# Splitting the products with the values into a high and a low step, with new figures in the plan that orders a two-layer attention kernel

## The chip, the cores and the metric

The kernel runs on one core of a Trainium2 chip. The metric is the device time of one execution in microseconds (us). Timed runs come without a profile; one further execution is recorded by the hardware profiler, and all stretches and durations below are of that one. Engines: PE is TensorE, PEld its weight loads, ACT ScalarE, DVE VectorE, POOL GpSimd, SP SyncE, which issues the DMAs.

## The reference, cut to what matters

Two layers over 1024 tokens of width 1024. Each normalises its input, multiplies it with one combined input weight, runs three groups of attention heads side by side, gates and concatenates their outputs, multiplies with an output weight, normalises and adds the residual.

```python
for l in range(DEPTH):
    h = rms_norm(x, pre_norm[l])
    (dq, dk, dv, dgate, gq, gk, gv, ggate, mq, mgate) = jnp.split(h @ w_in[l], IN_OFFSETS, axis=-1)
    oa = diff_attention(...)   # 6 heads: (softmax(q1 k1) - lam * softmax(q2 k2)) @ v
    ob = gqa_attention(...)    # 6 q heads on 2 kv heads: softmax(q k) @ v
    om = softmax(mq mk) @ mv   # 4 heads into 256 memory tokens
    y = jnp.concatenate([oa, ob, om], axis=-1) @ w_out[l]
    x = x + rms_norm(y, post_norm[l])
```

## The kernel before, in words

All large products are made of split operands: a number is kept as a high part and a low part, and high x high, high x low and low x high are added in PSUM. The softmax weights are split too. A unit is one PSUM tile of 128 x 1024 scores (pp). ScalarE takes its exponential into e (line 853, float32), ScalarE (rarely VectorE) rounds that to the high part eh (lines 857 and 858, float16), and GpSimd or VectorE subtracts to get the low part el (VectorE 859, GpSimd 860; the plan picks whichever it thinks is done first). Then `pv_part` multiplies with the values: for each block of 128 keys three products of 64 or 65 columns, eh with the values' high part (line 504), eh with the values' low part (505), el with the values' high part (506). The weights of each product are loaded anew. `pv_part` waits until all of its units have both parts, takes one 512-wide PSUM bank (ps), issues all its products as one piece of work, and ScalarE copies the result out (line 949).

An item is one head: "d" items (12 a layer, differential; units on line 1036), "g" items (6; units on 1250 and 1251) and "m" items (4, into the memory tokens; units on 1304 and 1305). Before an item's units the row maxima are needed: products on line 1026 (d), 1238 and 1239 (g) or 1293 and 1294 (m), reduced by VectorE on line 897, transposed on line 872, written by lines 878 and 879 and sent into the query operand by DMA. The m items share one pair of query operands, so the next m item's operands are fetched by DMA (big<-s_mqa, big<-s_gqb) only after the last unit of the m item before. The d items run beside the rest of the input projection (line 493), the g and m items after them, then the output product (line 1394).

The order on each engine is not the chip's choice. While the program is built, a plan in Python plays the kernel through: `use` gives each piece of work a duration on an engine, `LAT` a delay until others see its end, `KINDS` says how many PSUM tiles of each size each kind of work may hold and with which priority; a piece is written into the program at the moment at which the plan starts it. Each engine then runs its instructions strictly in that order. A changed figure in the plan thus reorders the whole program.

## Time and profile before

| | us |
|---|---|
| median of 3 runs | 1551.15 (1551.09 to 1554.43) |
| profiled execution | 1553.02 |
| its span, first to last instruction | 1551.2 |
| PE busy | 1487.1 |
| DVE, POOL, ACT busy | 1036.2, 903.0, 896.5 |

The profiled execution is 1.8 us longer than its span and 1.9 us longer than the median. PE's busy time is a union of overlapping products whose ends are modelled, so it is an upper bound of its work. PEclk is the granted TensorE clock as a share of 2.4 GHz: 1.00 is that, 0.50 is 1.2 GHz.

### The profile page before, as it was taken

The numbers are of one execution on the slowest core, as the hardware profiler recorded it, in microseconds if no ns is written. First come the engines' busy times: TensorE is split into PE (matmuls) and PEld (weight loads), VectorE is DVE, ScalarE is ACT, GpSimd is POOL, SyncE is SP. The second block draws the span as 40 slices with busy tenths as digits, with TensorE's granted clock in tenths as the row PEclk, the third lists the DMA queues.
The fourth block names the chain that finished last, engine by engine and source line by source line (L and its number), as shares of the span: only waits on it lengthen the run. The fifth ranks groups of instructions, "written<-read, shape, count | busy, mean of one in ns | idle before, by whom it ended". The sixth has DMA issues, their size and how long they took to land. (4 is left out here: it accounts for less than half of the span.)

```text
span 1551.2 us, 39344 instructions
## 1 busy us (share of the span) xinstructions
PE 1487.1 (96%) x15920; PEld 1375.1 (89%) x15920; DVE 1036.2 (67%) x2042; ACT 896.5 (58%) x1428; POOL 903.0 (58%) x647
## 2 busy tenths in 40 slices
PE   6999999999999999999999999999999998899997
PEld 5999999989999888888889999999899998788886
DVE  7747776788865886825566487776887757777143
ACT  4332668767668576673333346677657657576511
POOL 4133668789768486561122257678887757585500
PEclk9999999999999998999999999999999999899999
DMA  6435223233323644215254523223332156332242
GB/s 203 134 106 152 77 77 103 71 96 94 95 82 84 175 117 100 57 49 199 94 163 133 137 83 97 80 59 103 111 104 63 56 144 174 79 84 70 83 147 95
DMA packets 166048, 163.97 MB, mean 106 GB/s; under 512 B 14853, under 2 KB 140357, under 8 KB 165866
## 3 DMA queue, kind: packets, MB, share of 16 engines
q1 hardware_dynamic: 165866, 161.46, 35.7%
q8 instruction: 125, 2.05, 0.6%
q14 instruction: 57, 0.47, 0.1%
HBM read 110.96 MB, written 50.09 MB: 104 GB/s over the span
## 5 line engine op out<-in xcount | busy, mean ns | idle before, releaser
L860 POOL TENSOR_TENSOR el<-e,eh 128x1024 f16<-128x1024 f32 x258 | 570.0, 2221 | 208.0 <-ACT eh L857 194.7
L897 DVE TENSOR_REDUCE mx<-ps 128x1 f32<-128x512 f32 (+1 forms) x608 | 404.6, 684 | 145.6 <-PE ps L1026 86.8
L493 PE MATMUL ps<-wt,big 128*128 128x256 f32 x3456 | 490.0, 285 | 2.0 <-DVE nat L606 1.7
L493 PEld LDWEIGHTS ps<-wt,big 128*128 128x128 f32 x3456 | 465.0, 190 | 18.8 <-ACT e L853 2.0
L853 ACT ACTIVATE e<-pp 128x1024 f32<-128x1024 f32 x304 | 309.3, 1024 | 108.2 <-PE pp L1251 61.9
L857 ACT ACTIVATE eh<-e 128x1024 f16<-128x1024 f32 x262 | 275.4, 1057 | 2.4
L504 PEld LDWEIGHTS <-eh 128*128 128x128 f16 x2144 | 195.0, 96 | 14.4 <-issue 10.9
L394 POOL TENSOR_TENSOR wt<-rt,wt 128x512 fp32r<-128x512 f32 x89 | 123.7, 1401 | 136.6 <-ACT wt L392 96.0
L506 PEld LDWEIGHTS <-el 128*128 128x128 f16 x2144 | 196.6, 99 | 3.8 <-POOL el L860 3.4
L505 PEld LDWEIGHTS <-eh 128*128 128x128 f16 x2144 | 196.6, 97 | 0.7 <-issue 0.5
L436 POOL TENSOR_SCALAR u<-ss 128x1 f32<-128x1 f32 (+3 forms) x96 | 23.9, 249 | 253.3 <-DVE ss L1478 109.0
L493 PE MATMUL pp<-wt,big 128*128 128x256 f32 x1152 | 156.5, 291 | 8.8 <-POOL wt L394 4.1
L1026 PE MATMUL ps<-sdk,sdq 96*128 96x512 f32 x384 | 158.2, 413 | 3.9 <-DVE mx L897 2.4
L493 PEld LDWEIGHTS pp<-wt,big 128*128 128x128 f32 x1152 | 144.6, 194 | 11.7 <-POOL wt L394 4.9
L504 PE MATMUL ps<-vd,eh 128*128 128x65 f16 x1536 | 150.3, 193 | 0.2
L505 PE MATMUL ps<-vd,eh 128*128 128x64 f16 x1536 | 149.5, 194 | 0.0
L506 PE MATMUL ps<-vd,el 128*128 128x65 f16 x1536 | 149.0, 192 | 0.0
L1036 PE MATMUL pp<-sdq,sdk 98*128 98x256 f32 x768 | 125.8, 286 | 0.0
L1036 PEld LDWEIGHTS pp<-sdq,sdk 98*128 98x128 f32 x768 | 112.5, 190 | 5.3
L1250 PE MATMUL pp<-big 128*128 128x256 f32 x384 | 102.6, 297 | 0.3 <-ACT e L853 0.3
L1251 PE MATMUL pp<-big 67*128 67x256 f32 x384 | 100.3, 291 | 1.5 <-DMA big<-nl 1.5
L949 ACT ACTIVATE o<-ps 128x130 f32<-128x130 f32 (+1 forms) x160 | 46.1, 288 | 92.7 <-PE ps L506 91.8
(243 smaller groups left out, 2829.4 us busy)
## 6 DMA issues: line engine op xcount, KB each, us to landing
rt<-in_w_in SPq DMA_DIRECT2D x48, 256.0 KB
rt<-in_w_in SPq DMA_DIRECT2D x96, 128.0 KB
gt<-g_scr SPq DMA_DIRECT2D x32, 256.0 KB
rt<-in_w_out SPq DMA_DIRECT2D x32, 256.0 KB
sdq<-s_dqa SPq DMA_DIRECT2D x48, 128.0 KB
sdk<-s_dka SPq DMA_DIRECT2D x48, 128.0 KB
big<-s_gqa SPq DMA_DIRECT2D x24, 256.0 KB
big<-s_gqb SPq DMA_DIRECT2D x24, 256.0 KB
```

Source lines behind the costliest of these rows:

```text
L394: (POOL(512, lambda: pool.tensor_sub(out=lo, in0=rt, in1=raw(hi))), W_BIAS[1]))
L493: pe.matmul(ps, lhsT=x[:, kt, :], rhs=y[:, a, :], start=(kt == 0 and n == 0), stop=(kt == KT - 1 and n == 2))
L504: pe.matmul(o[:, 0:65], lhsT=eh, rhs=v[:, kt, 0:65], start=(kt == 0), stop=False, skip_group_check=True)
L505: pe.matmul(o[:, 0:64], lhsT=eh, rhs=v[:, kt, 66:130], start=False, stop=False, skip_group_check=True)
L506: pe.matmul(o[:, 0:65], lhsT=el, rhs=v[:, kt, 0:65], start=False, stop=(kt == n - 1), skip_group_check=True)
L853: yield ACT(1024, lambda: act.activation(e, ps, AF.Exp, scale=scale), 0, "p")
L857: yield either((ACT(1024, lambda: act.activation(eh, e, AF.Copy)), 0.0), (DVE(1024, lambda: dve.tensor_copy(out=eh, in_=e), 0, fast=True, ...
L860: (POOL(1024, lambda: pool.tensor_sub(out=el, in0=e, in1=eh)), 0.0))
L897: yield DVE(512, lambda: dve.tensor_reduce(out=out_ap, in_=src, axis=AX.X, op=ALU.max), MXP[0])
L1026: yield (512, lambda ps, n=n: pe.matmul(ps, lhsT=q()[0:96, i * P:(i + 1) * P], rhs=k()[0:96, n * 512:(n + 1) * 512], start=True, stop=True ...
L1036: pe.matmul(ps[:, a * 256:(a + 1) * 256], lhsT=k()[0:98, kt * P:(kt + 1) * P], rhs=q()[0:98, j * 256:(j + 1) * 256], start=True, stop=True)
L1250: pe.matmul(o, lhsT=ka()[:, ks], rhs=a()[:, qs], start=True, stop=False)
```

## The change

`attend` now makes either the two products with eh or the one with el. `pv_part` waits for the high parts alone, takes its bank, issues all high products of its query blocks, then waits for the low parts, and issues the low products as a second piece of work, with a priority (`PVL`, 0.1) ahead of the first's (`PVP`, 0.2). Since the blocks of one bank are now open at the same time, only the first product of the bank starts an accumulation. The kind "pv" may hold two banks in place of one, and `exp_part` fires one event for the high part and one for the low. The number of products and of weight loads is unchanged.

The plan's figures change: ScalarE's fixed part per instruction falls from 0.17 or 0.2 to 0.05 or 0.095 us, VectorE's from 0.13 to 0.08, PE's rate goes from 2210 to 2175 columns a us with small corrections for three kinds of work, and the plan now doubles PE's durations while its own account of PE's work says that the clock is low (`clocked`).

```diff
-DVE_FIX = 0.13
-PV_N = 2
+DVE_FIX = 0.08
+PV_AT, PVL = 0, 0.1
+PE_RATE, CLOCK_WINDOW, CLOCK_LOW, CLOCK_HIGH = 2175.0, 3.41, 0.33, 0.85
-KINDS = {... 'pv': (1, 1, 1), ...}
+KINDS = {... 'pv': (1, 2, 1), ...}
...
+        if eng == "pe":
+            dur = self.clocked(dur)
...
+    def clocked(self, dur):
+
+        while self.window < int(self.t / CLOCK_WINDOW):
+            share = self.work / CLOCK_WINDOW
+            self.half = share < (CLOCK_HIGH if self.half else CLOCK_LOW)
+            self.window += 1
+            self.work = max(0.0, self.work - CLOCK_WINDOW)
+        dur *= 2.0 if self.half else 1.0
+        self.work += dur
+        return dur
...
-        return use("pe", ncols / 2210.0, fn, prio, lat)
+        return use("pe", ncols / PE_RATE, fn, prio, lat)
...
-        return use("act", (0.2 if src == "s" else 0.17) + n / 1200.0, fn, prio)
+        return use("act", (0.095 if src == "s" else 0.05) + n / 1200.0, fn, prio)
...
-    def attend(o, v, es):
+    def attend(o, v, es, low, first):
...
+        for kt, e in enumerate(es):
+            if low:
+                pe.matmul(o[:, 0:65], lhsT=e, rhs=v[:, kt, 0:65], start=False, stop=(kt == n - 1),
+                          skip_group_check=True)
+            else:
+                pe.matmul(o[:, 0:65], lhsT=e, rhs=v[:, kt, 0:65], start=(first and kt == 0), stop=False,
+                          skip_group_check=True)
+                pe.matmul(o[:, 0:64], lhsT=e, rhs=v[:, kt, 66:130], start=False, stop=False, skip_group_check=True)
...
             for e in evs:
-                yield wait(e)
+                yield wait(e[PV_AT])
...
-            yield PE(sum(c for _, c in some) + 100, lambda: [f() for f, _ in some], PVP)
+            yield PE(sum(c for _, c in some) * 2 / 3 + 50, lambda: [f(0) for f, _ in some], PVP, 0.0)
+            for e in evs:
+                yield wait(e[1])
+            yield PE(sum(c for _, c in some) / 3 + 50, lambda: [f(1) for f, _ in some], PVL)
```

Two places in PE's order show it. The first is in layer 0, where units of the second m item (lines 1304 and 1305; 1330 and 1331 after) stand beside the products of a g item with the values (vg). Before, the three kinds of product alternate:

```order
L1305 MATMUL pp_75<-big 128x512
L504 LDWEIGHTS eh_1531
L504 MATMUL ps_78<-vg,eh_1531 128x65
L505 LDWEIGHTS eh_1531
L505 MATMUL ps_78<-vg,eh_1531 128x64
L506 LDWEIGHTS el_1532
L506 MATMUL ps_78<-vg,el_1532 128x65
```

Here and now the last high product (527), the unit with row maxima of a g item on either side of it (1264, 1265), and the first low product (522) of the same bank, ps_80:

```order
L527 LDWEIGHTS eh_1540
L527 MATMUL ps_80<-vg,eh_1540 128x64
L1264 MATMUL ps_79<-big 128x512
L1265 MATMUL ps_79<-big 128x512
L1330 MATMUL pp_75<-big 128x512
L1331 MATMUL pp_75<-big 128x512
L1330 MATMUL pp_75<-big 128x512
L1331 MATMUL pp_75<-big 128x512
L1264 MATMUL ps_77<-big 128x512
L1265 MATMUL ps_77<-big 128x512
L522 LDWEIGHTS el_1539
L522 MATMUL ps_80<-vg,el_1539 128x65
```

Eight products of 512 columns came between the parts of one group that stood together before. The second place, also on PE in layer 0, is where the row maxima of the fourth m item begin (1293 and 1294; 1319 and 1320 after). Before, they follow a g unit (1250, 1251), and both groups of products of the third m item with its values stand ahead of them:

```order
L1250 MATMUL pp_76<-big 128x256
L1251 MATMUL pp_76<-big 128x256
L1293 MATMUL ps_77<-big 128x256
L1294 MATMUL ps_77<-big 128x256
L1293 MATMUL ps_77<-big 128x256
```

Now the high products of the first such group, `vm` with ehm, and one g unit (1276, 1277) stand right ahead of them; its low products and the second group come later:

```order
L527 LDWEIGHTS ehm_8505
L527 MATMUL ps_79<-vm,ehm_8505 128x64
L1276 MATMUL pp_75<-big 128x256
L1277 MATMUL pp_75<-big 128x256
L1276 MATMUL pp_75<-big 128x256
L1277 MATMUL pp_75<-big 128x256
L1276 MATMUL pp_75<-big 128x256
L1277 MATMUL pp_75<-big 128x256
L1276 MATMUL pp_75<-big 128x256
L1277 MATMUL pp_75<-big 128x256
L1319 MATMUL ps_80<-big 128x256
L1320 MATMUL ps_80<-big 128x256
```

The row maxima moved forward, past half of the work that stood ahead of them. Counted over the whole program, VectorE makes 49 of the 304 low parts (16 before) and GpSimd 255 (288 before).

## Rows read from the trace of the kernel before

**Rows 1.** The page, its first part: busy time, share of the span and instructions of each engine.

```profile
PE 1487.1 (96%) x15920; PEld 1375.1 (89%) x15920; DVE 1036.2 (67%) x2042; ACT 896.5 (58%) x1428; POOL 903.0 (58%) x647
```

**Rows 2.** The page, its second part: busy tenths of PE and granted clock in 40 slices of 38.8 us.

```profile
PE   6999999999999999999999999999999998899997
...
PEclk9999999999999998999999999999999999899999
```

**Rows 3.** Who PE waited for over the whole span, longest first: us in total, times, longest.

```profile
PE ps L456 <- DVE xt L476: 8.2, 2, 5.4
PE ps L506 <- POOL elm L860: 6.5, 7, 1.8
PE pp L493 <- POOL wt L394: 4.1, 4, 1.6
PE pp L493 <- DVE nat L606: 4.0, 6, 1.2
PE ps L506 <- POOL el L860: 3.2, 2, 1.6
...
PE ps L1294 <- DMA big<-s_mqa: 2.8, 2, 2.1
PE ps L1026 <- DVE mx L897: 2.4, 2, 1.2
PE pp L1686 <- DMA grow<-in_pre_norm: 2.3, 1, 2.3
PE ps L1294 <- DMA big<-s_gqb: 2.0, 3, 1.1
...
PE ps L1293 <- DMA big<-s_mqa: 0.8, 2, 0.6
...
PE ps L1293 <- DMA big<-s_gqb: 0.4, 1, 0.4
```

**Rows 4.** Busy time of each engine by stretch (us from the span's start): length, then PE, PEld, DVE, ACT and POOL busy with counts, the granted clock, the DMA share and GB/s.

```profile
250.00:540.00 290.00, 286.41 (x3559) 272.48 (x3558) 215.45 (x406) 197.55 (x303) 220.70 (x149) 1.00 0.35 99
578.00:583.20 5.20, 2.12 (x50) 1.68 (x48) 3.37 (x4) 1.55 (x4) 2.27 (x2) 1.00 1.02 236
583.23:593.47 10.24, 10.24 (x41) 9.25 (x42) 5.82 (x13) 3.10 (x3) 1.53 (x1) 0.50 0.33 74
1298.00:1303.40 5.40, 3.81 (x74) 3.60 (x73) 5.40 (x6) 5.11 (x9) 4.94 (x3) 1.00 0.59 189
1303.44:1306.85 3.41, 3.41 (x47) 3.22 (x44) 2.46 (x3) 1.13 (x2) 3.41 (x2) 0.50 0.65 215
1306.90:1317.10 10.20, 7.49 (x105) 6.43 (x104) 4.43 (x6) 9.36 (x14) 7.97 (x5) 1.00 0.67 147
1317.10:1320.50 3.40, 3.40 (x18) 3.40 (x17) 2.65 (x5) 0.00 (x0) 2.45 (x2) 0.50 1.02 240
1342.00:1347.80 5.80, 3.73 (x99) 3.27 (x98) 5.14 (x5) 2.88 (x5) 4.04 (x2) 1.00 0.78 184
1347.82:1358.05 10.23, 9.10 (x37) 8.31 (x38) 5.06 (x10) 2.20 (x3) 0.29 (x1) 0.50 0.43 104
```

**Rows 5.** PE in order of time around the second m item of layer 0: start, us, engine, line, out<-in, shape, and in brackets the idle time before it.

```profile
573.76 0.20 PE L504 MATMUL ps<-vg,eh 128*128 128x65 f16 x1
...
575.20 0.19 PE L506 MATMUL ps<-vg,el 128*128 128x65 f16 x1
575.23 0.48 PE L1304 MATMUL pp<-big 128*128 128x512 f32 x1
...
576.01 0.39 PE L1305 MATMUL pp<-big 67*128 67x512 f32 x1
576.24 0.20 PE L504 MATMUL ps<-vg,eh 128*128 128x65 f16 x1
...
578.88 0.19 PE L504 MATMUL ps<-vm,ehm 128*128 128x65 f16 x1
580.99 0.19 PE L505 MATMUL ps<-vm,ehm 128*128 128x64 f16 x1
...
582.10 0.35 PE L1293 MATMUL ps<-big 128*128 128x256 f32 x1 [0.35 <-DMA big<-s_gqb]
583.20 0.58 PE L1294 MATMUL ps<-big 65*128 65x256 f32 x1 [0.74 <-DMA big<-s_gqb]
```

**Rows 6.** ACT and, last, POOL in order of time in the same stretch.

```profile
576.50 1.02 ACT L853 ACTIVATE e<-pp 128x1024 f32<-128x1024 f32 x1 [0.66 <-PE pp L1305]
577.55 1.06 ACT L857 ACTIVATE ehm<-e 128x1024 f16<-128x1024 f32 x1
...
578.74 2.12 POOL L860 TENSOR_TENSOR elm<-e,ehm 128x1024 f16<-128x1024 f32 x1 [0.59 <-ACT ehm L857]
```

**Rows 7.** PE in order of time elsewhere: the last unit of the first and third m items of layer 0 and of the first of layer 1 (1305), and the second operand's product of the next m item (1294).

```profile
546.37 0.40 PE L1305 MATMUL pp<-big 67*128 67x512 f32 x1
...
553.66 0.39 PE L1294 MATMUL ps<-big 65*128 65x256 f32 x1 [0.69 <-DMA big<-s_mqa]
...
611.86 0.40 PE L1305 MATMUL pp<-big 67*128 67x512 f32 x1
...
620.17 0.39 PE L1294 MATMUL ps<-big 65*128 65x256 f32 x1 [1.10 <-DMA big<-s_gqb]
...
1307.98 0.40 PE L1305 MATMUL pp<-big 67*128 67x512 f32 x1
...
1316.70 0.39 PE L1294 MATMUL ps<-big 65*128 65x256 f32 x1 [2.09 <-DMA big<-s_mqa]
```

**Rows 8.** Groups by line: count | busy us, mean ns of one | idle before it, and what ended it. ACT, POOL and DVE.

```profile
L392 ACT ACTIVATE wt<-rt 128x512 fp32r<-128x512 f32 x128 | 78.0, 627 | 15.7 <-DMA rt<-in_w_in 8.8 <-PE ps L493 2.2 <-PE pp L493 2.0
...
L860 POOL TENSOR_TENSOR el<-e,eh 128x1024 f16<-128x1024 f32 x258 | 570.0, 2221 | 208.0 <-ACT eh L857 194.7 <-POOL el L860 3.2 <-PE ps L1026 3.0
...
L859 DVE TENSOR_TENSOR el<-e,eh 128x1024 f16<-128x1024 f32 x10 | 15.7, 1570 | 12.0 <-POOL el L860 8.3 <-ACT eh L857 3.8
L859 DVE TENSOR_TENSOR elm<-e,ehm 128x1024 f16<-128x1024 f32 x6 | 12.1, 2025 | 0.0
```

**Rows 9.** ACT and PE in order of time at the start of the program: three ACT instructions of one line in a row, and 24 and 10 products of line 493 in a row.

```profile
8.01 1.66 ACT L392 ACTIVATE wt<-rt 128x512 fp32r<-128x512 f32 x3
...
23.44 3.12 PE L493 MATMUL pp<-wt,big 128*128 128x256 f32 x24
...
26.75 1.44 PE L493 MATMUL pp<-wt,big 128*128 128x256 f32 x10
```

More of the change, by code (lines that the diff above doesn't have):

```diff
@@ L74 @@
 LAT = {"pe": 0.231, "act": 0.176, "dve": 0.165, "pool": 0.121, "hwdge": 0.65, "dma": 0.95}
-DVE_FIX = 0.13
-PV_N = 2
+DVE_FIX = 0.08
+PV_AT, PVL = 0, 0.1
 X_GATE, XT = 2, 4
 DMA_RATE = 300.0
+PE_RATE, CLOCK_WINDOW, CLOCK_LOW, CLOCK_HIGH = 2175.0, 3.41, 0.33, 0.85
 SLACK = 0.8
-KINDS = {'un': (0.5, 2, 2), 'z': (1, 2, 2), 's0': (2, 2, 2), 's1': (0, 2, 2), 'st': (1, 4, 1), 'pv': (1, 1, 1), 'tr': (-1, 2, 1), 'mx': (2, 4, 1), 'zh': (3, 2, 1)}
+KINDS = {'un': (0.5, 2, 2), 'z': (1, 2, 2), 's0': (2, 2, 2), 's1': (0, 2, 2), 'st': (1, 4, 1), 'pv': (1, 2, 1), 'tr': (-1, 2, 1), 'mx': (2, 4, 1), 'zh': (3, 2, 1)}
 def raw(t):
@@ L192, in __init__ @@
         self.port = {"dve": 0.0, "pool": 0.0}
+        self.window, self.work, self.half = 0, 0.0, False
         self.live = 0
@@ L494, in f @@
                                   stop=(kt == KT - 1 and n == 2))
-            yield PE(6 * NC, f, prio, None if j == 3 else 0.0)
+            yield PE(6 * NC * 1.015, f, prio, None if j == 3 else 0.0)
             if last and wi is not None:
                 free("wt", wi)
-    def attend(o, v, es):
+    def attend(o, v, es, low, first):
         n = len(es)
-        for kt, (eh, el) in enumerate(es):
-            pe.matmul(o[:, 0:65], lhsT=eh, rhs=v[:, kt, 0:65], start=(kt == 0), stop=False, skip_group_check=True)
-            pe.matmul(o[:, 0:64], lhsT=eh, rhs=v[:, kt, 66:130], start=False, stop=False, skip_group_check=True)
-            pe.matmul(o[:, 0:65], lhsT=el, rhs=v[:, kt, 0:65], start=False, stop=(kt == n - 1),
-                      skip_group_check=True)
+        for kt, e in enumerate(es):
[6 more added lines that the diff above has]
+                pe.matmul(o[:, 0:64], lhsT=e, rhs=v[:, kt, 66:130], start=False, stop=False, skip_group_check=True)
     class Layer:
@@ L858, in exp_part @@
                          (DVE(1024, lambda: dve.tensor_copy(out=eh, in_=e), 0, fast=True, port=True), HI_BIAS[kind]))
+            box.append((eh, el, ei))
+            ev[0].fire(pl)
             yield either((DVE(1024, lambda: dve.tensor_sub(out=el, in0=e, in1=eh), port=True), LO_BIAS[kind]),
@@ L861, in exp_part @@
             free("e32", n32[1])
-            box.append((eh, el, ei))
-            ev.fire(pl)
+            ev[1].fire(pl)
         def nm_rows(mx, n2, scale, dst, ready):
@@ L972, in stream @@
                     yield PE(ncols, lambda: mm(ps), UNP)
-                    box, ev = [], Event()
+                    box, ev = [], (Event(), Event())
                     pl.spawn(exp_part(ps, slot, it.scale, kind, box, ev, (e32, k)))
@@ L992, in pv_list @@
                     es.append((eh[:, o:o + P], el[:, o:o + P]))
-                out.append((lambda c=66 * i, es=es: attend(ps[:, c:c + 65], v, es), 201 * nk))
+                out.append((lambda low, c=66 * i, es=es: attend(
+                    ps[:, c:c + 65], v, [e[low] for e in es], low, c == 0), 198 * nk))
             return out
@@ L1037, in f @@
                                   rhs=q()[0:98, j * 256:(j + 1) * 256], start=True, stop=True)
-                return 1024, f
+                return 1040, f
             it.loads, it.max_parts, it.unit_mm = loads, max_parts, unit_mm
@@ L1397, in z_mm @@
                         end = k == KT_ORDER[-1] and h == 1
-                        yield PE(3 * 512, f, prio, None if end else 0.0)
+                        yield PE(3 * 512 * 0.98, f, prio, None if end else 0.0)
                         used.append(t)
```

## The prediction

> **What bounds the kernel now.** First the busy times: PE is busy for 1487.1 of the span's 1551.2 us, no other engine for more than 67% [rows 1]. So the kernel is bound by PE's work, and the change, which leaves the number of products and weight loads as it is, can only win what PE loses: 1551.2 - 1487.1 = 64.1 us of idle time, and what PE loses inside its busy time at the lower clock. The slices show where: PE is at six tenths in the first one, and the only two with a clock below nine tenths of full, at 582 and 1318 us, lie once in each layer, in the stage of the g and m items; the second of them and its neighbour are also the only ones before the end with PE at eight tenths [rows 2]. Third, whom PE waits for: the low parts el of the softmax weights for 6.5 + 3.2 = 9.7 us in nine waits; the query operands of the m items for 2.8 + 2.0 + 0.8 + 0.4 = 6.0 us; at the program's start normalised input and the gain for 8.2 + 2.3 = 10.5 us; the rest is spread over many waits, weight parts and rotated projections the longest of them [rows 3]. Fourth, the stretches: four at the granted clock 0.50 (1.2 GHz), 583 to 593, 1303 to 1307, 1317 to 1321 and 1348 to 1358; in front of each PE was busy for 41% to 73% only, while in a d stage, 250 to 540, it was busy for 286.4 of 290 us and the clock stayed at 1.00 [rows 4].
>
> **The change part by part.** Durations first. A product of 256 columns takes (3.12 - 1.44)/14 = 0.12 us from start to start [rows 9], one of 512 columns 576.24 - 576.01 = 0.23 us, one with the values 0.031 us (48 of them take 575.23 - 573.76 = 1.47 us) [rows 5]. With these I count how much PE work stands in an order between two places; PE's own idle time there comes on top, so the counts are lower bounds of the distances.
>
> *The wait for el.* The place to see it: PE is through with the last product of a unit of the second m item at 576.24, its exponential starts at 576.50, the high part is done at 577.55 + 1.06 = 578.61, the low part on GpSimd at 578.74 + 2.12 = 580.86, and PE, which stopped after 578.88, goes on at 580.99 [rows 5, 6]. So with nothing in the way el can be used 580.99 - 576.24 = 4.75 us after its unit, and eh, with the same 0.1 us of handing over, 2.5 us after it. In PE's old order 14 of the 160 groups stand closer than 4.75 us behind their unit, the closest 2.3 us. In the new one three low steps do (4.69 us in each layer, 2.84 us once): 0.1 + 1.9 = 2.0 us are left. The high steps are new waits: three of 160 stand closer than 2.5 us (2.22 us in each layer, 1.85 us once), 1.1 us in all. This term: -9.7 + 2.0 + 1.1 = -6.6 us; bounds -9.7 and, if the high steps wait as the low ones did, 0.
>
> *The clock.* The four stretches at 0.50 hold 10.24 + 3.41 + 3.40 + 9.10 = 26.15 us of busy PE [rows 4], half of which full clock would save: 13.1 us. Ahead of the first stands the wait for el above, 2.1 us; but waits for the m operands stand there too (583.20 in [rows 5], 1316.70 in [rows 7]), and those the change does not touch. I take half, -6.5 us; bounds -13.1 and 0.
>
> *The m operands.* From the start of the last product of an m item's units to the second operand's product of the next item, PE took 7.3, 7.2 and 8.3 us in layer 0 and 8.7 us in the first case of layer 1 [rows 5, 7]: the DMAs start only after that unit, whatever else PE does. Take 7.2, less 0.23 for that product and 0.12 for the first operand's, 6.85 us of other work to be found. The old order has 4.8, 3.0 and 5.8 us, the new one 4.6, 6.2 and 3.9 (the last: 48 high and 16 low products, and two g units of eight products of 256 columns). That leaves 2.2 + 0.6 + 2.9 = 5.7 us of waiting a layer, 11.5 in all, where 6.0 is waited now [rows 3]: **+5.5 us**; bounds 0 (PE idles in between for other reasons, as it did for el) and +9 (8.3 in place of 7.2 us in three of six).
>
> *The plan's figures.* Three ScalarE instructions of 0.627 us [rows 8] take 1.66 us in a row [rows 9], (1.66 - 0.63)/2 = 0.52 from start to start. The old figure for them is 0.2 + 512/1200 = 0.63, the new one 0.095 + 0.43 = 0.52: the old plan held ScalarE busy 0.1 us too long with every instruction, the new one does not. Orders laid out on true times should make PE wait less at places where it now waits for ACT, DVE and POOL. The idle time outside el, m operands and start is 64.1 - 9.7 - 6.0 - 10.5 = 37.9 us. No row shows what a better figure wins, and at the layer seams and the end there is no other work to put in; I take -2 us, a twentieth. Bounds: -12, a third of it, and +8, since tighter distances leave less room for what the plan has no figure of, DMA and the port that DVE and POOL share by the plan's own account (el on DVE takes 1570 to 2025 ns here, POOL's 2221 [rows 8]).
>
> *Edits at no cost.* The 33 low parts that go from POOL to DVE add 33 x 1.74 = 57 us to DVE and take 33 x 2.22 = 73 us from POOL; neither sets the end [rows 1]. What queues behind them on DVE is the reduction of the row maxima; PE waits 2.4 us for it now [rows 3], and four small banks cover more; uncovered, that wait again, +2.4. The second bank does nothing in steady work: in the new order high and low steps strictly alternate, since a group still waits for the one before it; it only spares the wait for ScalarE's copy out of the first. The start of the program is reordered too (ScalarE squares the first tile before it copies the gain, VectorE makes more of the input tiles ahead of the low parts): 0, within 3 us either way, of the 8.2 us there [rows 3].
>
> The sum against the profiled execution: 1553.0 - 6.6 - 6.5 + 5.5 - 2.0 = 1543.4 us. The median of the runs is 1.9 us below the profiled execution, so the forecast for the median is **1541.5 us**, 0.6% faster.
>
> **The rivals.**
>
> *The high step waits for ScalarE (slower).* In the d stages ScalarE is busy for 197.6 of 290 us [rows 4]. If one of its other instructions stands in the way, eh comes not 2.5 but 3 to 3.5 us after the unit (one rounding of 1.06 us [rows 6] in its way). Summed over the new order, PE waits 1.1 us for the high parts if they take 2.5 us, 8 us at 3.0 and 25 us at 3.5: the gain of 9.6 us is gone from about 3.1 us on, and at 3.5 the time is 1541.5 + 24 = 1565. For it: 46 of the 96 high steps of the d items stand within 4 us of their unit, where the closest group stood 5.5 us off before. Against it: the plan lets a high step start only when its own ScalarE is done, and its figure for that engine now agrees with the rows.
>
> *The waits change places (no change).* The el waits shrink by 6.6 us, the m operands take 5.5 more, and since it is those that stand in front of the low stretches, the clock falls as often as now: 1553.0 - 6.6 + 5.5 = 1551.9, less 1.9, 1550. For it: the last DMA wait ends 0.03 us before the stretch at 583.23 [rows 4, 5].
>
> *The figures matter more (much faster).* All four low stretches go (-13.1), the better distances win 12 us, and the m operands cost what the sum above has: 1553.0 - 6.6 - 13.1 + 5.5 - 12 = 1526.8, less 1.9, 1525.
>
> *The clock falls at the new seams (slower).* Each group now has a seam between two steps at which PE can stand for a moment. The trace so far speaks against it: in the d stage the groups follow one another through the four small banks at 1.00 [rows 4]. If it happened at three seams a layer, each time for 10.24 us as at 583 and losing half of them, it would cost 6 x 5.1 = 31 us: 1541.5 + 31 = 1572; for 3.4 us each, 10 us: 1552. The Trainium skill, "TensorE: Matmul & The Clock Gate", section "A second HAM failure mode: psum-queue depth-cycling", has a rule that speaks for this rival: a kernel that cycled its products through PSUM banks idled so often between groups that its clock went back and forth between the two levels. By that rule the second bank and the split harm; by the row above, cycling banks did not harm here as long as the work was there.
>
> **How the numbers follow.** A measurement of this kernel can tell about 0.3% from no change, so faster is below 1546.5 and slower above 1555.8. The forecast, with its own range 1534 to 1550, gets 0.48, of which 0.40 faster, 0.07 the same and 0.01 slower; waits that change places 0.19 (0.02, 0.13, 0.04); much faster 0.17; the high step 0.12; the seams 0.04. That makes 0.59 faster, 0.20 the same, 0.21 slower. The range of 1527 to 1558 leaves out half of the much faster case and most of the two slower ones, some 0.2; the bounds of the terms (clock -13.1, operands +9, figures -12 to +8) fill it.
>
> **What would show it.** In the profile after, the waits of the low products for el should come to some 2 us, those of the high products for eh to less; if the high ones are above 10 us, the first rival holds. The waits of lines 1319 and 1320 for the m operands should be near 11 us. Of the four stretches at 0.50 about half should be gone. PE's busy time should fall by the clock's share alone, some 6 us, to about 1480, with the same 15920 products; more idle time at the layer seams or in the d stages than now would prove the term of the figures wrong.

## The result, and the profile after

| | before | after |
|---|---|---|
| median, us | 1552.79 (4 runs, 1551.09 to 1555.79) | 1572.85 (4 runs, 1572.26 to 1572.92) |
| ratio | | 1.0126, interval 1.0107 to 1.0145 |
| span of the profiled execution, us | 1551.2 | 1571.1 |

The change makes the kernel 20 us slower; 1541.5 us had been forecast, 0.6% faster, and the range ended at 1558. After each line of before stands its new number here: 456, 493, 1026, 1238, 1293, 1294 and 1686 [rows 3] are 472, 509, 1052, 1264, 1319, 1320 and 1712; the products with the values are 525 and 527 (high parts) and 522 (low parts).

The page of after, its first part and PE's row of the second:

```profile
PE 1505.9 (96%) x15920; PEld 1377.7 (88%) x15920; DVE 1059.4 (67%) x2079; ACT 892.2 (57%) x1428; POOL 830.2 (53%) x610
...
PE   6999999999999999999989999999999998999997
```

With the same 15920 products PE is busy 18.8 us longer than in [rows 1], where some 6 us less were expected: the first sign that PE's own work had become dearer. The idle time, 1571.1 - 1505.9 = 65.2 us, hardly moved from 64.1. Whom PE waited for in after, over the whole span (us in total, times, longest):

```profile
PE ps L472 <- DVE xt L492: 9.7, 4, 4.2
PE ps L509 <- DVE nat L626: 6.1, 4, 1.6
PE ps L472 <- DVE hn L492: 5.2, 2, 3.7
PE ps L1264 <- DVE gs L711: 4.0, 2, 2.5
PE ps L509 <- DVE nl L901: 3.5, 2, 1.8
PE ps L1319 <- DMA big<-s_gqb: 3.0, 2, 1.9
...
PE ps L1320 <- DMA big<-s_gqb: 1.6, 2, 0.9
...
PE ps L1320 <- DMA big<-s_mqa: 1.0, 2, 0.5
...
PE ps L525 <- ACT ehm L878: 0.7, 2, 0.4
...
PE ps L522 <- DVE el L882: 0.2, 1, 0.2
```

The 9.7 us of waits for low parts [rows 3] are down to 0.2, and the waits for high parts come to 0.7. The m operands cost 3.0 + 1.6 + 1.0 = 5.6 us, as much as before (6.0). In their place stand waits for VectorE: for rotated projections (nat), the normalised input of layer 1 (hn), gates (gs) and row maxima (nl). All rows of this view that name VectorE add up to 42.4 us; in the trace of before they add up to 23.7.

Now PE in order of time in layer 0 (start, us, line, out<-in, shape): the end of a high step, four products of a unit, the low step, and the next unit.

```profile
560.09 0.19 PE L527 MATMUL ps<-vg,ehm 128*128 128x64 f16 x1
560.12 0.48 PE L1330 MATMUL pp<-big 128*128 128x512 f32 x1
560.43 0.40 PE L1331 MATMUL pp<-big 67*128 67x512 f32 x1
560.67 0.40 PE L1330 MATMUL pp<-big 128*128 128x512 f32 x1
560.91 0.40 PE L1331 MATMUL pp<-big 67*128 67x512 f32 x1
561.15 0.66 PE L522 MATMUL ps<-vg,elm 128*128 128x65 f16 x16
561.65 0.48 PE L1330 MATMUL pp<-big 128*128 128x512 f32 x1
561.97 0.40 PE L1331 MATMUL pp<-big 67*128 67x512 f32 x1
```

The first 512-column product behind value products takes 560.43 - 560.12 = 0.31 us to the next start, the second and third 0.24; behind the low step again 0.32. No engine is waited for there. It is a price for the seam itself, about 0.08 us, and the split makes a group pay it about twice.

To add up such prices I took, for every product of a trace, the time from its start to the next start, less the median for its shape in the trace of before, and sorted these excesses by place. Products in the first 20 us and at the low clock are kept apart; elsewhere an excess above 0.15 us counts as a wait, whatever the place.

| excess of PE, us | before | after | difference |
|---|---|---|---|
| float32 product behind a value product | 10.2 (122 places) | 21.7 (260) | +11.5 |
| value products among themselves | -0.1 | 5.3 | +5.4 |
| first value product of a group | 1.5 | 3.1 | +1.6 |
| waits above 0.15 us | 58.8 | 61.1 | +2.3 |
| at the low clock | 16.3 | 12.9 | -3.4 |
| behind transposes, start, all else | 24.6 | 27.1 | +2.5 |
| sum | 111.3 | 131.2 | +19.9 |

The sum is the 20 us that the span grew by. This is bookkeeping on two traces: what each part does to the time when it alone is taken away, the experiments below have to tell. The first three rows, 18.5 us, are what I call PE's own time below; the other two that matter are waits and low clock.

### The profile page after: what moved, and what is told of

Its sections match the earlier page's. It is cut to its first block, busy times and chain, and to the rows that moved or that the text cites. A ratio compares the mean times of both kernels' runs of the same rounds, so it can differ in the third digit from the quotient of the medians.

```text
span 1571.1 us, 39318 instructions
## 1 busy us (share of the span) xinstructions
PE 1505.9 (96%) x15920; PEld 1377.7 (88%) x15920; DVE 1059.4 (67%) x2079; ACT 892.2 (57%) x1428; POOL 830.2 (53%) x610
## 3 DMA queue, kind: packets, MB, share of 16 engines
q8 instruction: 125, 2.05, 0.6%
## 4 chain that ended last, share of the span: by engine, by line
PE 72%; DVE 10%; DMA 6%; issue 5%; ACT 3%; POOL 2%; SPq 1%; POOLq 0%; ACTq 0%; DVEq 0%
PE ps L509 21%; PE pp L1420 8%; PE pp L509 5%; PE ps L1052 5%; PE pp L1062 5%; PE ps L522 4%; PE ps L525 4%; PE ps L527 4%; DVE mx L919 3%; PE ps L1264 2%; PE pp L1276 2%; PE pp L1277 2%; PE ps L1265 2%; SPq L346 1%; PE ps L1420 1%
## 5 line engine op out<-in xcount | busy, mean ns | idle before, releaser
L883 POOL TENSOR_TENSOR el<-e,eh 128x1024 f16<-128x1024 f32 x235 | 516.1, 2210 | 182.5 <-ACT eh L878 156.8
L509 PE MATMUL ps<-wt,big 128*128 128x256 f32 x3456 | 495.6, 287 | 11.6 <-DVE nat L626 6.1
L874 ACT ACTIVATE e<-pp 128x1024 f32<-128x1024 f32 x304 | 309.5, 1027 | 126.2 <-PE pp L1062 65.9
L410 POOL TENSOR_TENSOR wt<-rt,wt 128x512 fp32r<-128x512 f32 x81 | 114.4, 1421 | 145.1 <-ACT wt L408 106.0
L1052 PE MATMUL ps<-sdk,sdq 96*128 96x512 f32 x384 | 162.1, 422 | 5.2 <-DVE nat L626 1.5
L525 PEld LDWEIGHTS <-eh 128*128 128x128 f16 x2144 | 138.5, 98 | 16.9 <-issue 10.7
L527 PEld LDWEIGHTS <-eh 128*128 128x128 f16 x2144 | 140.5, 98 | 0.1
L525 PE MATMUL ps<-vd,eh 128*128 128x65 f16 x1536 | 110.6, 194 | 0.9 <-DVE nat L626 0.9
L527 PE MATMUL ps<-vd,eh 128*128 128x64 f16 x1536 | 109.7, 193 | 0.0
L408 ACT ACTIVATE wt<-rt 128x512 fp32r<-128x512 f32 x128 | 78.7, 629 | 38.0 <-DMA rt<-in_w_in 23.9
L1264 PE MATMUL ps<-big 128*128 128x512 f32 x192 | 84.1, 438 | 4.2 <-DVE gs L711 4.0
L711 DVE SCALAR_TENSOR_TENSOR gs<-sq,ps 128x256 f32<-128x256 f32 x64 | 26.6, 416 | 91.1 <-ACT sq L703 72.9
```

The source lines that it names most:

```text
L509: pe.matmul(ps, lhsT=x[:, kt, :], rhs=y[:, a, :], start=(kt == 0 and n == 0), stop=(kt == KT - 1 and n == 2))
L525: pe.matmul(o[:, 0:65], lhsT=e, rhs=v[:, kt, 0:65], start=(first and kt == 0), stop=False, skip_group_check=True)
L527: pe.matmul(o[:, 0:64], lhsT=e, rhs=v[:, kt, 66:130], start=False, stop=False, skip_group_check=True)
L874: yield ACT(1024, lambda: act.activation(e, ps, AF.Exp, scale=scale), 0, "p")
L883: (POOL(1024, lambda: pool.tensor_sub(out=el, in0=e, in1=eh)), 0.0))
L1052: yield (512, lambda ps, n=n: pe.matmul(ps, lhsT=q()[0:96, i * P:(i + 1) * P], rhs=k()[0:96, n * 512:(n + 1) * 512], start=True, stop=True ...
```

## The experiments

All numbers in one table first. Medians are of 4 to 12 runs; the ratio is to runs of the kernel before made beside them (medians 1550.3 to 1553.3 us), while differences in the text are against 1551.2. Own time, waits and low clock are the sums above, and the last two columns add up the rows of the view of waits that name VectorE, and those that name eh, ehm, el or elm.

| kernel | median, us | ratio (interval) | own | waits | low clock | for VectorE | for eh, el |
|---|---|---|---|---|---|---|---|
| before | 1551.2 | 1 | 11.6 | 58.8 | 16.3 | 23.7 | 9.7 |
| one step: ScalarE's figure | 1555.5 | 1.0032 (1.0017-1.0047) | 10.9 | 59.2 | 12.7 | 32.6 | 7.4 |
| one step: VectorE's figure | 1545.4 | 0.9962 (0.9949-0.9975) | 9.8 | 49.4 | 15.9 | 30.2 | 11.2 |
| one step: PE's figures and clock | 1554.3 | 1.0024 (1.0006-1.0042) | 11.8 | 60.8 | 12.9 | 36.1 | 9.0 |
| one step: rate 2200 | 1554.5 | 1.0016 (0.9996-1.0037) | 11.3 | 53.2 | 23.0 | 24.5 | 14.6 |
| one step: rate 2245 | 1568.9 | 1.0118 (1.0087-1.0150) | 10.8 | 75.5 | 12.5 | 45.0 | 8.9 |
| one step: all new figures | 1576.9 | 1.0155 (1.0124-1.0185) | 10.9 | 75.4 | 16.4 | 54.3 | 0.5 |
| two steps: all new figures (after) | 1572.9 | 1.0126 (1.0107-1.0145) | 30.1 | 61.1 | 12.9 | 42.4 | 0.9 |
| two steps: old figures | 1561.3 | 1.0074 (1.0053-1.0095) | 31.1 | 56.8 | 6.3 | 25.2 | 9.5 |
| two steps: VectorE's figure | 1558.3 | 1.0041 (1.0023-1.0059) | 29.5 | 53.0 | 7.4 | 27.2 | 7.7 |
| two steps: rate 2200 | 1575.1 | 1.0167 (1.0141-1.0192) | 29.2 | 64.6 | 17.1 | 25.7 | 11.2 |
| two steps: rate 2245 | 1600.0 | 1.0316 (1.0287-1.0345) | 31.6 | 80.9 | 19.4 | 48.7 | 5.6 |
| two steps' products in one, low parts last | 1582.7 | 1.0193 (1.0161-1.0224) | 16.4 | 71.6 | 15.4 | 51.0 | 0.0 |
| after, grouped | 1568.4 | 1.0115 (1.0087-1.0143) | 22.0 | 66.3 | 8.5 | 41.3 | 1.4 |
| one step, VectorE's figure, grouped | 1546.2 | 0.9960 (0.9943-0.9978) | 7.8 | 55.1 | 16.0 | 29.2 | 8.0 |
| after, joined late | 1608.4 | 1.0371 (1.0351-1.0391) | 18.0 | 92.7 | 20.4 | 62.1 | 0.5 |
| after, joined late, grouped | 1603.0 | 1.0328 (1.0297-1.0358) | 10.2 | 91.3 | 23.7 | 60.0 | 0.7 |
| old figures, joined late, grouped | 1556.9 | 1.0044 (1.0030-1.0059) | 11.0 | 65.9 | 7.8 | 40.0 | 4.1 |
| VectorE's figure, joined late, grouped | 1562.0 | 1.0067 (1.0039-1.0094) | 9.5 | 67.4 | 5.6 | 35.1 | 2.7 |

### Steps and figures apart

Two steps on old figures: in the changed kernel all the plan's figures go back, the corrections for kinds of work too, and `clocked` is not called.

```diff
-DVE_FIX = 0.08
+DVE_FIX = 0.13
...
-PE_RATE, ... = 2175.0, ...
+PE_RATE, ... = 2210.0, ...
...
-            dur = self.clocked(dur)
+            pass
...
-        return use("act", (0.095 if src == "s" else 0.05) + n / 1200.0, fn, prio)
+        return use("act", (0.2 if src == "s" else 0.17) + n / 1200.0, fn, prio)
...
```

> The split in two steps and two banks, with the figures of the plan before. Theory S (seams): the split itself costs: PE needs 0.083 us more for the first float32 product behind a group of float16 value products, and the order has 276 such seams against 128 before and 266 after; with slower float16 products the time is 1552.8 + 148 x 0.083 + 8 - 9 (el) = 1564, up to 1573. Theory W (waits of the new order): the figures make the loss, so without them the split wins its el waits: 1552 or below, near 1545.

One step on all new figures is the kernel before with the opposite of that diff, and so with one bank for the products with the values.

> The new figures with the products with the values in one step as before; 114 seams in the order. Theory S: 1552.8 - 1.2 for 14 seams fewer, and whatever the figures bring, within 1545 to 1558. Theory W: the loss of the change comes from the order that the figures make: 1565 or above.

Two steps' products in one, low parts last, is the changed kernel with one PE piece a group, which waits for both parts, high products first; the second bank stays:

```diff
-PV_AT, PVL = 0, 0.1
+PV_AT, PVL = 1, 0.1
...
-            yield PE(sum(c for _, c in some) * 2 / 3 + 50, lambda: [f(0) for f, _ in some], PVP, 0.0)
-            for e in evs:
-                yield wait(e[1])
-            yield PE(sum(c for _, c in some) / 3 + 50, lambda: [f(1) for f, _ in some], PVL)
+            yield PE(sum(c for _, c in some) + 100, lambda: [f(k) for k in (0, 1) for f, _ in some], PVP)
```

> The changed kernel, but a group waits for its low parts first and issues high products and low products as one piece, 116 seams. Theory S: 150 seams fewer than in the changed kernel, 1572.9 - 150 x 0.083 = 1560, less again if the float16 products are only slow at their starts, plus el waits of up to 5: 1553 to 1563. Theory W: the order is still one of the new figures, 1567 or above. The difference to the run without the split tells what the order of products in a group costs: 0 to 7 us.

Measured: 1561.3, 1576.9 and 1582.7 us. The first came out near theory S (1564), the other two where theory W had them (1565 or above, 1567 or above). Neither half is harmless: the two steps alone cost 10 us, the figures alone 26, and together they cost not 36 but 22 against the same 1551.2. On the new figures, two steps and one are not clearly told apart (1572.9 and 1576.9, intervals that overlap). The third run has its seams gone (own time 30.1 to 16.4), but it is a new order too, with waits at 71.6, and is slower than after. Two things come out of this. The wait for el was in the main not the steps' to give: it goes with the new figures and one step, while with the two steps on the old figures 9.5 us stay, more than half of them as a wait of the high products:

```profile
PE ps L525 <- ACT eh L878: 5.4, 8, 0.9
PE ps L522 <- POOL el L883: 3.1, 8, 0.5
```

And what the figures cost is waiting for VectorE, 54.3 us in place of 23.7. The longest rows of one step on new figures that name it (the first is hardly above the 8.2 of before; sl is the low part of transposed projections):

```profile
PE ps L472 <- DVE xt L492: 8.7, 3, 5.9
PE ps L472 <- DVE hn L492: 5.3, 2, 3.7
PE ps L509 <- DVE nat L622: 5.1, 2, 2.6
PE ps L520 <- DVE sl L687: 4.0, 2, 2.0
```

### The seam by itself

A small kernel repeats PE work only, in five arrangements of 12 products of 256 columns (line 63) and one group of 48 value products, 16 rounds each.

```diff
+    for _ in range(16):
+        wide(12); trio("a", 0); trio("a", 1)
+    for _ in range(16):
+        wide(6); high("b", 0); high("b", 1)
+        wide(6); low("b", 0); low("b", 1)
+    for _ in range(16):
+        wide(12); high("c", 0); high("c", 1); low("c", 0); low("c", 1)
+    for _ in range(16):
+        wide(6); trio("d", 0)
+        wide(6); trio("d", 1)
```

In the fifth, for each block all products with the high halves of the values stand first, then those with the low halves, then the low parts.

> No attention: TensorE alone on loaded tiles, five blocks of 16 rounds, each round with 12 float32r products of 256 columns and 48 float16 products in another arrangement: a, one group in the order eh x high, eh x low, el x high; b, 6 wide, 32 high, 6 wide, 16 low; c, 12 wide, 32 high, 16 low; d, 6 wide, 24 in the order of a, twice; e, 12 wide, then per half 8 eh x high, 8 eh x low, 8 el x high. The output is not the reference's. Theory S: a round takes 12 x 0.12 + 48 x 0.0305 + 0.09 = 3.0 us in a, 0.09 more in d, 0.09 plus about 0.05 more in b, 0.05 more in c. Theory W: all five within 0.03 us of each other.

PE in order of time, the wide products alone: two starts of a, three of b (the middle one is the break inside its round), two of c, three of d (the middle one likewise), two of the fifth.

```profile
34.31 1.67 PE L63 MATMUL rr<-xr 128*128 128x256 f32 x12
...
37.28 1.67 PE L63 MATMUL rr<-xr 128*128 128x256 f32 x12
...
100.70 0.96 PE L63 MATMUL rr<-xr 128*128 128x256 f32 x6
...
102.52 0.96 PE L63 MATMUL rr<-xr 128*128 128x256 f32 x6
...
103.81 0.96 PE L63 MATMUL rr<-xr 128*128 128x256 f32 x6
...
137.78 1.68 PE L63 MATMUL rr<-xr 128*128 128x256 f32 x12
...
140.80 1.68 PE L63 MATMUL rr<-xr 128*128 128x256 f32 x12
...
195.44 0.95 PE L63 MATMUL rr<-xr 128*128 128x256 f32 x6
...
196.98 0.95 PE L63 MATMUL rr<-xr 128*128 128x256 f32 x6
...
198.51 0.95 PE L63 MATMUL rr<-xr 128*128 128x256 f32 x6
...
229.07 1.67 PE L63 MATMUL rr<-xr 128*128 128x256 f32 x12
...
232.02 1.19 PE L63 MATMUL rr<-xr 128*128 128x256 f32 x8
```

All rounds of an arrangement are alike. The same work takes 37.28 - 34.31 = 2.97 us a round with one break, 3.07 with two and the same product order (d), 3.02 with one and high products ahead of low ones (c), and 3.11 as the change has it (b). So a break costs 0.10 us, the order in which eh meets vh and vl (the values' high and low parts) in turn 0.05, the split of one group 0.14. In PE's order of after a float32 product stands behind a value product 266 times, in that of before 128 times: 138 x 0.14 = 19 us, where the accounting has 18.5. The fifth arrangement is the cheapest, 2.95.

### One figure at a time

Each is the kernel before with one edit: ScalarE's figure, VectorE's, PE's with the clock and the corrections for kinds of work, and two rates that are no truer than the old one.

```diff
-        return use("act", (0.2 if src == "s" else 0.17) + n / 1200.0, fn, prio)
+        return use("act", (0.095 if src == "s" else 0.05) + n / 1200.0, fn, prio)
```

> The kernel before with one of the new figures alone: ScalarE's fixed part (0.2 and 0.17 us become 0.095 and 0.05). Both steps of the change, the clock and the other figures are left out. Theory F (one figure misleads the planner, and ScalarE's is the largest of the change): this one holds most of the loss that all the new figures brought together, 1566 to 1578 us. Theory R (any new order of this program loses, because the figures of the kernel before happen to give a good one; the change of a figure is a new draw): 1556 to 1570 us, and about the same as the other single figures and as the neutral figure. Theory N (this figure is harmless): 1549 to 1555 us.

```diff
-DVE_FIX = 0.13
+DVE_FIX = 0.08
```

> The kernel before with VectorE's fixed part alone changed (0.13 us becomes 0.08). Theory F with VectorE as the culprit (in the changed kernel TensorE's waits are for VectorE): 1566 to 1578 us, and the ScalarE figure alone harmless. Theory R (a new draw of the order): 1556 to 1570 us. Theory N (harmless): 1549 to 1555 us.

```diff
-        return use("pe", ncols / 2210.0, fn, prio, lat)
+        return use("pe", ncols / PE_RATE, fn, prio, lat)
...
+        if eng == "pe":
+            dur = self.clocked(dur)
...
```

> The kernel before with TensorE's figures alone changed: the rate 2175, the three sizes by kind of product, and the planner's model of the clock. Theory F with the clock model as the culprit: 1566 to 1578 us, both other single figures harmless. Theory R (a new draw): 1556 to 1570 us. Theory N: 1549 to 1555 us; here the low-clock stretches of the record would also be fewer than in the kernel before.

```diff
-        return use("pe", ncols / 2210.0, fn, prio, lat)
+        return use("pe", ncols / 2245.0, fn, prio, lat)
```

> The kernel before with TensorE's rate in the plan at 2245 where it stood at 2210: as large a step as the change's, in the other direction, and with no other edit; it says nothing truer of the chip. It changes the order of nearly all of TensorE's work. Theory R (any new draw of the order loses against the one that the kernel before has): 1556 to 1570 us. Theory F (a particular new figure misleads the planner): 1548 to 1556 us, since none of them is here.

The last one was run again later with 2200 in place of 2245:

> The kernel before with TensorE's rate in the plan at 2200 where it stood at 2210: half of one per cent, and no other edit. Theory R (any change of a figure draws a new order, and a draw is worth -6 to +26 us): 1545 to 1577 us, and off the kernel before by more than 5 us. Rival (the time follows the size of the figure's error, so a small step does little): 1548 to 1555 us.

Measured: +4, -6, +3, +18 and +3 us against 1551.2. Theory F (one misleading figure) fell: the three parts add up to about 2 us where all together cost 26, and a step of 1.6% in a rate, with no new figure, costs 18. Theory R in its strict form (every new order loses) fell too: three of the five are within 5 us and one gains. Of the last one the rival was right: the step of half of one per cent moved the time by 3 us, 1.2 against the kernel before as run beside it. What stands is weaker: the figures give other orders of the whole program, and six such orders of the same work (these five and one step on all new figures) lie between -6 and +26 us. The waits of the 2245 kernel, longest first, show the kind of loss:

```profile
PE ps L456 <- DVE xt L476: 8.2, 2, 5.4
PE pp L1251 <- DMA big<-nl: 6.9, 2, 3.8
PE ps L662 <- DVE nat L606: 6.6, 5, 2.2
PE ps L493 <- DVE nat L606: 6.5, 4, 2.1
...
PE ps L493 <- DVE vg L597: 4.9, 4, 1.4
```

VectorE again (45.0 us), here most of all for projections that it rotates (nat). Its load is not the cause: it is busy 1044.0 us here, 1081.2 in the fastest kernel, where PE waits 30.2 us for it.

### The same figures with the two steps

The two steps and the second bank on VectorE's figure and on each rate complete five pairs. In all of them the two steps come with the second bank and the low step's priority; what these do by themselves was not tried.

```diff
-DVE_FIX = 0.13
+DVE_FIX = 0.08
```

> The two steps of the changed kernel (with two banks) on the plan's figures of the kernel before, with VectorE's fixed part alone at 0.08 us: the figure that, without the two steps, gave 1545.4 us. Theory R (each set of figures is a new draw of the order, and nothing of it carries over; the two steps cost 17 us of seams and product order and give back some 10 us of waits for low parts): anywhere from 1552 to 1578 us. Rival (VectorE's figure is simply truer and the two steps are near neutral): 1543 to 1550 us.

```diff
-PE_RATE, ... = 2210.0, ...
+PE_RATE, ... = 2245.0, ...
```

> The two steps of the changed kernel on the figures of the kernel before with TensorE's rate at 2245, the neutral figure that gave 1568.9 us without the two steps. Theory R (a new draw): 1552 to 1578 us, as likely below 1568.9 as above. Rival (2245 is a worse figure by 17 us in itself, and the two steps add some 8 to it): 1574 to 1582 us.

```diff
-PE_RATE, ... = 2210.0, ...
+PE_RATE, ... = 2200.0, ...
```

> The two steps of the changed kernel on the old figures with TensorE's rate at 2200: the fifth pair with and without the two steps on the same figures. The four so far differ by +10, -4, +13 and +31 us. Theory (the two steps cost on average, some 18 us of seams and product order less some 9 of waits, with a draw on top): 0 to 25 us above its partner. Rival (they are neutral or gain, and three of the four were draws): 0 to 20 us below its partner.

Measured: 1558.3, 1600.0 and 1575.1 us. The two steps against one, by pair: old +10, new -4, VectorE's +13, 2245 +31, 2200 +21, on average +14 with an interval of about 16 either way, so a cost in time is likely from these pairs but not certain. What is certain is the own time: it rises in all five pairs by 18 to 21 us; the rest, waits and clock, scatters between -23 and +10. The waits for eh and el change by +0.4 to -3.5 us from one step to two on the same figures. The 2245 pair fitted neither expectation: the two steps lost more than the rival had it, with 80.9 us of waits.

### Product order with nothing drawn anew

In the changed kernel, and in the kernel with VectorE's figure and one step, the products inside a piece are put in another order; every piece stays in its place.

```diff
...
+        for kt, e in enumerate(es):
+            pe.matmul(o[:, 0:65], lhsT=e, rhs=v[:, kt, 0:65], start=bool(not low and first and kt == 0),
+                      stop=bool(low and kt == n - 1), skip_group_check=True)
+        for kt, e in enumerate(es if not low else ()):
+            pe.matmul(o[:, 0:64], lhsT=e, rhs=v[:, kt, 66:130], start=False, stop=False, skip_group_check=True)
```

> The changed kernel with one edit inside its steps: in the high step all products with the values' high halves of one row block come first, then all with their low halves, where they stood in turn. The order of all steps on all engines stays that of the changed kernel, so nothing is drawn anew. Theory P (the order of the short products costs 57 ns a step of 32, as in the measurement of the seams, where 1019 + 494 ns in two pieces and 1502 in one fell to 1445): 128 steps by 57 ns are 7.3 us, so 1563 to 1568 us where the changed kernel takes 1572.9. Rival (the short products' extra nanoseconds are covered by waits elsewhere in the program): 1571 to 1574 us.

> The kernel before with VectorE's fixed part at 0.08 us (1545.4 us so far), and one edit inside its one step of value products: all products of the high parts first (of a row block, those with the values' high halves, then those with the low halves), the low parts' products last, in the same piece and with no seam between. The order of all steps on all engines stays that of that kernel. Theory P (product order gives 128 by 18 ns, 2.3 us, and the wait for low parts, 10.4 us in the record of that kernel, is mostly covered by the 32 products ahead, about 1 us each time, so some 4 to 7 us more): 1536 to 1540 us. Rival (what the low parts' wait gives up comes back as other waits, as in the changed kernel): 1543 to 1546 us.

Measured: 1568.4 us, 4.4 less than after, and 1546.2, no gain on 1545.4. The own time fell as expected (30.1 to 22.0, and 9.8 to 7.8), but waits rose by 5.2 and 5.7 us: work that PE does sooner makes it wait sooner. Of the gain in PE's own time about half came back in the one (with 4.4 us less lost at the low clock), all in the other, where the rival had 1543 to 1546. The second is the fastest kernel but one, and not told from it.

### High products at the low step's place

The plan and the order of all else stay; the high step puts nothing out, and the low step puts out both.

```diff
-            yield PE(sum(c for _, c in some) * 2 / 3 + 50, lambda: [f(0) for f, _ in some], PVP, 0.0)
+            yield PE(sum(c for _, c in some) * 2 / 3 + 50, lambda: None, PVP, 0.0)
...
-            yield PE(sum(c for _, c in some) / 3 + 50, lambda: [f(1) for f, _ in some], PVL)
+            yield PE(sum(c for _, c in some) / 3 + 50, lambda: [f(k) for k in (0, 1) for f, _ in some], PVL)
```

> The changed kernel with the high step's products put out where its low step stands, in one piece with them; the plan and the order of every other step stay as they are, so nothing is drawn anew, and a group of value products has one seam where it had two (266 places where a float32 product follows value products become 140). Theory S (a seam costs its 0.083 us in the program too): 126 x 0.083 + some 1.3 for the dearer first product of a group, 12 us less: 1557 to 1564 us. Rival (TensorE waits in those places anyway, or the later high products make others wait): 1569 to 1576 us.

The three others have the grouped product order as well, on the new figures, the old ones, and VectorE's.

> As the run before it, and with the value products of a piece grouped (high parts by the values' high halves, high parts by their low halves, low parts last). Theory S with theory P: 12 us for the seams and 8 for the product order, as the record of the grouped kernel had them: 1549 to 1557 us. Rival (half of such a gain comes back as other waits, as it did in the grouped kernel): 1558 to 1566 us.

> The changed kernel on the plan's old figures (1561.3 us), with the same two edits: high products at the low step's place, and grouped. Nothing is drawn anew against that kernel. Theory S with theory P: 124 seams by 0.083, 1.3 and 8 us less: 1538 to 1547 us, faster than the kernel before. Rival (half comes back): 1548 to 1556 us.

> The two steps on the old figures with VectorE's fixed part at 0.08 us (1558.3 us), with the same two edits. Nothing is drawn anew against that kernel. Theory S with theory P: 120 seams by 0.083, 1.2 and 8 us less: 1535 to 1544 us. Rival (half comes back): 1546 to 1553 us.

Measured: 1608.4, 1603.0, 1556.9 and 1562.0 us. On the new figures theory and rival both failed: the times are 32 and 37 us beyond the rival's. The seams did go (own time 30.1 to 18.0), but waits rose from 61.1 to 92.7 and the low clock from 12.9 to 20.4. The stretch from 250 to 540 us, busy time of PE, PEld, DVE, ACT and POOL, then the clock; first after, then the joined kernel:

```profile
250.00:540.00 290.00, 283.45 (x3331) 267.21 (x3330) 194.20 (x404) 180.58 (x291) 202.35 (x142) 0.99 0.35 98
```

```profile
250.00:540.00 290.00, 276.73 (x3353) 260.38 (x3351) 187.97 (x387) 181.10 (x287) 200.23 (x139) 0.99 0.32 87
```

PE stands for 13.3 us in a stretch in which it stood for 6.6 in after and 3.6 before [rows 4]. Its waits in the joined kernel that grew or are new:

```profile
PE ps L1264 <- DVE gs L711: 6.2, 2, 3.1
PE ps L1052 <- DVE mx L919: 5.2, 11, 1.1
...
PE ps L1052 <- DVE nat L626: 3.8, 6, 1.0
...
```

All rows that name VectorE come to 62.1 us, 42.4 in after. The eleven waits for mx, none above 1.1 us, would fit this reading: the 32 high products, 1.0 us, used to stand between VectorE's order and PE's use of its result, and without them the result comes too late. The order with them in another place was not followed result by result, so it stays a reading. On the old figures the joined kernel gained 4.4 us of the 20.1 that its own time fell by, a quarter and not the rival's half (1548 to 1556; measured 1556.9); on VectorE's figure it lost 3.7, with 20.0 us less of own time, and theory and rival both failed.

## Why the prediction was wrong

**The step that failed first: a cost that it did not have.** The sum started from "the number of products and weight loads as it is" and put the split under edits at no cost; the only price that it gave a seam was the clock's. The seams and the order of eh with vh and vl cost 18.5 us of PE's own time in the record, 19 by the small kernel, 18 to 21 in each of five pairs. [rows 5] had it: the float32 product at 575.23 stands behind a value product, and its 0.48 us beside 0.39 at 576.01 was a hint. With this term alone the forecast would have been 1560. That own time turns into time one for one is not shown: where the order was held and the added seams taken out (in three of four kernels the dear product order too), own time fell by 12 to 20 us and the time changed by -4 to +36, since other waits came up.

**The plan's figures: -2 us, bounds -12 to +8.** The prediction's own sign against this term came: in the d stage from 250 to 540 us PE stood for 6.6 us where it had stood for 3.6 before. Outside the waits for eh and el, waits rose from 49.1 to 60.2 us, +11; the figures cost 12 us with the two steps (1561.3 to 1572.9) and 26 without. Here a term of unknown sign was given a gain because the new figures fit the rows better, and too narrow bounds. The runs show six orders of the same work from -6 to +26 us, the second worst from a rate that was only moved by 1.6%. Whether truer figures are of any use, they don't show; they do show that fitting the rows promised nothing. (The bounds also leaned on DMA and the port as things that the plan has no figure of; it has one for each, `DMA_RATE` and `port`.) Why all the new figures together lose when each alone does not is open.

**The wait for el: -6.6 us, measured -8.8.** The count of distances in the new order was near. But it is the order that the new figures give that took the wait away, and not the two steps: it goes with one step on the new figures (0.5 us), and with two steps on the old ones 9.5 of 9.7 us stay.

**The clock: -6.5 us, measured -3.4.** Half of the low stretches were to go; there are six ahead of the end, as many as before, where two in the first 170 us stood beside the four of [rows 4]. They are shorter, 30.7 us in place of 34.1. In after (length, the engines' busy times, then the clock):

```profile
214.46:217.87 3.41, 3.41 (x17) 3.22 (x16) 2.46 (x5) 0.49 (x2) 0.00 (x0) 0.50 0.27 78
525.07:531.90 6.83, 6.36 (x24) 5.78 (x25) 3.42 (x6) 0.77 (x2) 0.00 (x0) 0.50 1.03 222
627.47:634.30 6.83, 6.22 (x29) 6.22 (x30) 4.38 (x5) 2.93 (x3) 3.83 (x2) 0.50 0.36 88
801.55:804.97 3.42, 2.94 (x14) 2.94 (x15) 2.66 (x4) 1.63 (x3) 2.82 (x4) 0.50 0.50 161
989.29:992.70 3.41, 3.41 (x16) 3.22 (x15) 2.34 (x5) 0.28 (x1) 0.00 (x0) 0.50 0.28 79
1310.14:1316.97 6.83, 5.42 (x17) 4.46 (x18) 5.61 (x13) 2.81 (x5) 5.56 (x6) 0.50 0.59 169
```

Ahead of each or across its start, PE's timeline has a wait of 1.8 to 3.7 us: for row maxima (nl, nm) at 211, 987 and 1309 us, for a gate at 523, for an m operand at 625, for hn at 798; none for a part of the softmax weights. So the waits for el were gone, as forecast, and five of the six stretches stand at waits for VectorE instead.

**The m operands: +5.5 us, measured -0.4.** The term set a count for the new order against a measured wait of the old one. Counted the same way the old order has 2.05 + 3.85 + 1.05 = 6.95 us a layer, 13.9 in all, more than twice the 6.0 that were measured; like for like, count against count, the forecast was a fall of 2.4 us. In layer 0 of after, the last product of three m items' units (1331) and the second operand's product of the next (1320):

```profile
562.44 0.39 PE L1331 MATMUL pp<-big 67*128 67x512 f32 x1
...
569.02 0.38 PE L1320 MATMUL ps<-big 65*128 65x256 f32 x1 [0.53 <-DMA big<-s_mqa]
...
587.87 0.40 PE L1331 MATMUL pp<-big 67*128 67x512 f32 x1
...
595.04 0.28 PE L1320 MATMUL ps<-big 65*128 65x256 f32 x1
...
620.56 0.40 PE L1331 MATMUL pp<-big 67*128 67x512 f32 x1
...
628.08 0.58 PE L1320 MATMUL ps<-big 65*128 65x256 f32 x1 [0.72 <-DMA big<-s_gqb]
```

With the 1.9 us that 1319 waits ahead of the last (the longest of its row in the waits above), the three waits are 0.5, 0 and 2.7 us where 2.2, 0.6 and 2.9 were counted. The work in between took 0.6 to 0.9 us longer than the count has it, with 0.2 us of other idle time at most, and once the operands were there after 6.6 us and not 7.2.

**The rivals.** The high steps did not wait (0.7 us): the first fell in after, though on the old figures it came about in part (5.4 us). "The waits change places" was true of waits as such, +2.3 us net. The rival of the clock at new seams gave 1552 to 1572 and so nearly the right time for a wrong reason: seams do cost, but in PE's own time at full clock. The rule cited beside it, from the Trainium skill, "TensorE: Matmul & The Clock Gate", section "A second HAM failure mode: psum-queue depth-cycling", is not borne out here: with twice the seams and a second bank the low clock cost 12.9 us instead of 16.3, and with the steps on the old figures 6.3. In four of the five pairs the two steps lose less at the low clock than one step does; with the rate 2245 they lose more (19.4 against 12.5).

## What to carry to other kernels

Count the places where PE changes from one kind of product to another before a piece of work is split: a split that changes no product can still cost 0.14 us each time, 0.10 for the break and the rest for the order inside, and the starts of neighbouring products show where. Where a plan lays out the order of a program whose PE is busy for 96% of the time, a changed figure can be a new draw, whatever its truth; give it the spread of several neutral draws as bounds, and judge an edit by pairs on several sets of figures or with the order held. When a price counted in one order is set against a wait measured in another, count both orders first. Small pieces that seem to be in the way may be what covers another engine's delay.

## What the runs showed of the hardware

- The first float32 product behind a short float16 product takes about 0.08 us longer to the next start (0.31 instead of 0.24 in after, 11.5 us over 138 more places); one more change there and back costs 0.10 us a round in the small kernel. Behind transposes the excess is about as large. What makes it was not tried.
- Value products of 64 or 65 columns, each with its own weight load, follow one another in some 0.03 us, and their order matters: 48 of them take 0.05 us more with eh meeting vh and vl in turn ahead of the low parts than in threes, and 0.02 less when grouped by halves of the values.
